# Block 1's attention: fewer chunks projected up front, a second buffer for the written parts, and operands loaded one head ahead

## The chip, the cores and the metric

The kernel runs on one core of one Trainium2 chip. The metric is the time of one execution on the device, in microseconds (us). The core has five engines that run side by side and wait for each other by semaphores: TensorE (PE, matmuls and transposes into PSUM), VectorE (DVE), ScalarE (ACT), GpSimd (POOL) and SyncE (SP), which here issues nearly all DMAs. PSUM has eight banks of 128 x 512 float32; the kernel calls them a to h.

## The reference, cut to what matters

Three blocks work one after the other on x, 512 tokens of 1024 features, float32. Each mixes tokens and then applies a feed-forward layer. The change lies in the mixer of the first block, which has two kinds of attention side by side:

```python
h = rms_norm(x, mix_norm[l])
proj = h @ w_in[l]
qa, ka, va, qb, kb, vb = [proj[..., offs[i]:offs[i + 1]] for i in range(6)]
...
oa = diff_attention(qa[:, :, 0], qa[:, :, 1], ka[:, :, 0], ka[:, :, 1], va, lam, rel_bias)
oa = rms_norm(oa, diff_subln[l]) * (1.0 - lambda_init)
...
qb = apply_rope(rms_norm(qb, q_norm[l]), cos, sin)   # shortened
kb = apply_rope(rms_norm(kb, k_norm[l]), cos, sin)   # shortened
ob = gqa_attention(qb, kb, vb)
x = x + jnp.concatenate([oa, ob], axis=-1) @ w_out[l]
```

There are 8 differential heads (two maps of scores each, with a bias by distance, whose difference weighs the values) and 8 grouped heads, four of which share one of two key and value heads. A head is 64 wide.

## The kernel before, in words

Activations lie with their features on the partitions, as eight chunks of [128, 512 tokens]. A matmul in float32 is made of three matmuls of float32r: each operand is cut into a high and a low part (hi on ACT, lo on DVE), and hi*hi + hi*lo + lo*hi is summed in PSUM (`mm3x`, L116 to L122). A weight panel comes by DMA into `wraw`, a ring of three, and is cut into `whi` and `wlo` at L137 and L138. A projection of one chunk (`proj`) is 8 x 3 = 24 matmuls of 512 columns.

`heads1` (L538 to L696) is the attention of block 1. Its order before the change:

1. The two grouped key heads are projected, normed and rotated (`rope(4, "kpd", "mm")`, function at L544).
2. For chunks 0 and 1, which are two heads of each kind: the differential q and k (`proj_q`, `proj_k`, L643 to L647) and the grouped q (`rope`) are projected, through the PSUM ring "mm" (banks a to f).
3. Sixteen heads follow in turns, a differential one (d) and a grouped one (g): d0, g0, d1, g1 and so on; chunk c holds the heads 2c and 2c+1. Within the heads stand the value projections (`v_tokens`, at the first grouped head, 192 matmuls of 320 columns through banks c to f) and the projections of chunks 2 and 3: q and k at the first grouped head of chunk c - 2, the grouped q at the second differential head of chunk c - 2. These use the kind "pj", bank h alone.

`AH = 2` (L39) says how many chunks are projected ahead.

The result of each of these projections is drained by DVE (`af` at L582, `rf` at L550), and `parts` (L463) writes its two parts to DRAM, to be set out anew on the partitions:

```python
hl = self.keep("hl", self.HL, F32R, w=1024).rearrange("p (a w) -> p a w", a=2)   # L466
nc.scalar.activation(hl[:, 0], f, AF.Copy)                                       # L468
nc.vector.tensor_sub(hl[:, 1], f, f32v(hl[:, 0]))                                # L469
d = self.dr.tile([128, 2, 512], F32, name=name, tag=name, bufs=4)                # L473
nc.sync.dma_start(out=d, in_=f32v(hl))                                           # L474
```

`HL = 1` (L40): there is one such buffer. (Block 3 sets it to 2 for itself at L1412.) A head's operands are then loaded from DRAM: `operand` (L585) makes `qd` and `kd` of a differential head by three DMAs each, from the ring "op1" of three buffers (L589 issues); `keys` (L568) loads the shared grouped keys, `kg`, two buffers, four DMAs at L573; the grouped q, `qg`, comes by two DMAs at L665. All of these are issued by SP, whose queue runs in order.

The heads are run by `attend` (L406). A head's four units (128 queries each) make the scores: for a differential head at L602, with bias and row minimum on DVE at L604 and the exponential on ACT at L460; for a grouped one at L626, L627 and L460. A head's unit runs ahead of the values of the head before: `values` (L429) transposes the weights on TensorE (L437, banks c and d), cuts them (`pth` L445, `ptl` L446) and multiplies them with the values (L447, L448, L441, banks e and f); `fold` (L456) adds the halves. A head's operands are loaded when its first unit is written (`lazy`, L634, calls `mk_diff` or `mk_gqa`).

After the heads stands the first half of the output's projection (`half_res`, L522), eight projections of 12 matmuls in bank h. Each is tied by `issue_after` (L531) behind a matmul of the heads' values, the first behind one of the tenth head, the last behind one of the sixteenth.

The order on each engine is not written out by hand. The kernel is a list of instructions whose place gives their priority; a scheduler with a model of their costs lays them out at build time, as their operands become ready in that model, and a tile waits until a buffer of its ring is free. So a projection can run well before or after its place in the list, but on each engine the order is then fixed, and an instruction that waits holds up all behind it.

Temporary tiles of 128 x 512 come from a ring of five, "u", and for four names (`dq`, `pf`, `ct`, `cacc`, used in block 2) from a ring of three, "v", both in one pool that lives through the whole kernel (L78 to L82).

Of the kernel before, what the change touches and what calls it, by code (L numbers as in the profile page):

```python
# [21 lines left out]
# vectors with a column or more per partition, that come in one array  # L22
# [11 lines left out]
class K:  # L34
# [4 lines left out]
    AH = 2  # L39
    HL = 1  # L40
# [37 lines left out]
    def t(self, name, dt=F32):  # L78
        """A [128, 512] tile that lives for a few instructions."""
        if name in self.SECOND:  # L80
            return self.tp.tile([128, 512], dt, name=name, tag="v", bufs=3)
        return self.tp.tile([128, 512], dt, name=name, tag="u", bufs=self.NU)  # L82

    def ld(self, name):
        """One that is loaded from DRAM, ahead of its use."""
        return self.tp.tile([128, 512], F32, name=name, tag="ld", bufs=self.NL)

    def tx(self, name):
        """The same in the place of the residual's parts, when those are done."""
        return f32v(self.keep(name, 16, F32R, self.xp, tag="x"))  # L90
# [15 lines left out]
    def psum(self, kind="mm"):  # L106
        """A bank of PSUM; kinds that share none don't wait for each other."""
        ring = self.BANKS[kind]
        tag = ring[self.turn.get(kind, 0) % len(ring)]
        self.turn[kind] = self.turn.get(kind, 0) + 1  # L110
        return self.ps.tile([128, 512], F32, name=tag, tag=tag, bufs=1)
# [12 lines left out]
    def weight(self, src, n, nk, own=0):  # L124
        """Load a weight panel [128, nk*128] and cut it into two parts."""
# [21 lines left out]
    def weight_bg(self, src):  # L147
        """The same for work beside the main line, 512 columns at a time."""
# [9 lines left out]
    def split_act(self, x, name, bufs, scale=None):  # L158
        """x (times a per-partition scale) into two float32r parts."""
# [12 lines left out]
    def rsqrt(self, p, w, scale, eps=EPS, own=False):  # L172
        """1/sqrt(p*scale + eps) of [128, w] sums, rounded like float32; eps may be a tile."""
# [7 lines left out]
        # the exponent and mantissa bits give log2 within 0.043; two Newton steps follow  # L181
# [7 lines left out]
    def tok_sums(self, st, s, ind, n, nq=4):  # L189
        """Sums over s's partitions by token: st[:, q*n + j] = sum_p s[p, q*128 + token] ind[p, j];  # L190
        s may be a list, whose sums are added."""
# [5 lines left out]
    def rows(self, r, kind="mm"):  # L197
        """[128 tokens, 4] -> the tokens' row on all partitions (PSUM)."""
# [5 lines left out]
    def head_rows(self, r, split, kind="mm"):  # L204
        """r[:, q, h] of some heads -> rows of a chunk whose partitions are (half, head, 32) or (head, d)."""
# [19 lines left out]
    def rstd(self, acc, dim=1024, kind="st", own=False):  # L225
        """1/sqrt(mean+eps) by token from the sums of squares acc, [128 tokens, 4]."""
# [4 lines left out]
    def on_rows(self, r, kind="mm"):  # L231
        """The same on all partitions, [128, 512 tokens]."""
# [10 lines left out]
    def feed_start(self, g):  # L243
        """The residual's chunks arrive one by one; the next phase gets them normed by g."""
# [14 lines left out]
    def feed_end(self):  # L259
        """The fed chunks, 1/sqrt(mean+eps) of each token by row and by column, the residual."""  # L260
# [18 lines left out]
    def aside(self, ph, f, *args):  # L279
        """Calls f with its tiles in the pool ph."""  # L280
# [13 lines left out]
    def start(self, g):  # L294
        """The kernel's input as a phase gets it, its chunks on chip; the first weights come before."""
# [69 lines left out]
    def bias_rows(self):  # L365
        """-rel_bias of every key - query in DRAM, one copy per partition."""
# [39 lines left out]
    def attend(self, heads):  # L406
        """Heads as (unit, values, odd, dst, done): unit(q) makes the scores of a query
        chunk and returns a function that gives the weights; a head's units run ahead of
        the values of the one before."""
# [19 lines left out]
    def values(self, pv, kc):  # L429
        """o += v^T p^T for one chunk of keys; both parts of v on o's rows."""  # L430
# [19 lines left out]
    def fold(self, o, odd, dst):  # L450
        """Sum of the two 64-row halves of o into the even or odd half of dst."""
# [6 lines left out]
    def soft(self, p, mx, sm, e):  # L458
        """exp(-p - max(-p)) with its row sums."""
# [3 lines left out]
    def parts(self, f, name, scale=None):  # L463
        """A chunk's two parts in DRAM, to be set out anew on the partitions."""
# [15 lines left out]
    def v_tokens(self, src, xhl, vt, rtok, nh):  # L480
        """Values with tokens on partitions, each head as (hi | lo)."""
# [40 lines left out]
    def half_res(self, ocs, gs, res):  # L522
        """The residual and the output's projection of the first halves of both kinds of heads, in DRAM."""
# [14 lines left out]
    def heads1(self, xhl, rb, rtok, gq, ind, ocs):  # L538
# [5 lines left out]
        def rope(c, name, kind="pj"):  # L544
            """Grouped attention's q (or its k): projection, norm, gain and rotation of a
            chunk, whose rows are the first halves of its two heads and then the second
            halves; both parts of it in DRAM."""
# [20 lines left out]
        def keys(kv):  # L568
            ds = []
            for i in range(2):  # L570
                t = self.keep("kg", 2, F32R)
# [5 lines left out]
        # values  # L577
# [7 lines left out]
        def operand(tag, d, r, order):  # L585
            """The two 32-row groups of a head as 96-row operands of both parts."""
            t = self.keep(tag, 3, F32R, tag="op1", w=1024).rearrange("p (r w) -> p r w", r=2)
# [4 lines left out]
        def diff_head(h, sms, q2, k2):  # L592
# [4 lines left out]
            def unit(q):  # L597
# [9 lines left out]
                def weights():  # L607
                    """The two maps' difference, times the first one's sum."""
# [39 lines left out]

        def mk_diff(c, r):
            if r == 1:  # L650
                qgd[c + self.AH] = rope(c + self.AH, "qpd") if c < 4 - self.AH else None
            return diff_head(2 * c + r, sms[c], operand("qd", qds[c], r, (0, 0, 1)), operand("kd", kds[c], r, (0, 1, 0)))

        def mk_gqa(c, r):
            if r == 0:
                if c == 0:
                    self.v_tokens(D["w1_v"], xhl, vt, rtok, 5)
                if c % 2 == 0:
                    kg[c // 2] = keys(c // 2)
                if c < 4 - self.AH:  # L660
                    proj_q(c + self.AH)
                    proj_k(c + self.AH)
            t = self.keep("qg", 2, F32R)
            for i in range(2):
                nc.sync.dma_start(out=f32v(t[64 * i:64 * i + 64]), in_=self.part_rows(qgd[c], i, 32 * r, [(64, 2), (1, 32)]))  # L665
            return gqa_head(r, sms[4 + c], t, kg[c // 2])

        kg = {}
# [16 lines left out]

        for c in range(self.AH):
            proj_q(c, "mm")
            proj_k(c, "mm")
            qgd[c] = rope(c, "qpd", "mm")
# [9 lines left out]
    def tok_proj(self, src, lhs, nk, n, ntok, evac, kind="mm"):  # L699
        """Tokens on partitions: [128 ntok, n] blocks of x @ w, w as the moving operand."""  # L700
# [11 lines left out]
    def mod_start(self):  # L712
        """silu of c and c_ctx, doubled, on all partitions."""
# [13 lines left out]
    def mod_step(self, m):  # L727
        """A chunk of c @ w_mod (and of c_ctx's), features on partitions."""
# [11 lines left out]
    def modulation(self):  # L740
        """silu(c) @ w_mod + b_mod for c and c_ctx, features on partitions."""
# [19 lines left out]
    def log_decay(self):  # L761
        """log_sigmoid of the decay logits on all partitions, [128, (direction, head)]."""
# [7 lines left out]
        # log1p(e) = 2 atanh(e / (2 + e))  # L770
# [16 lines left out]
    def ctx_normed(self):  # L787
        """The context, normed and modulated, in two parts, and the decays over its positions."""
# [25 lines left out]
        # decays over the context's positions, with k's scale  # L814
# [11 lines left out]
    def ctx_states(self, hl, dec):  # L826
        """The two states that the context leaves, per head [128 d, 128 e], in two parts."""
# [23 lines left out]
    def norm_mod(self, xs, gg, sh, scale_b):  # L851
        """h = x * gg * scale_b + sh, in two parts."""
# [12 lines left out]
    def acc_sq(self, acc, s, c):  # L865
        """The squares of 8 chunks added up, the last ones left apart."""
# [1164 lines left out]
```

## Time and profile before

| | before |
|---|---|
| median of 3 runs | 2702.98 us |
| lowest and highest | 2700.18 and 2704.9 us |
| span of the profiled execution | 2697.9 us |
| PE busy in that span | 2605.0 us |
| DVE busy | 1565.2 us |
| ACT busy | 1053.6 us |
| DMA, mean | 126 GB/s |
| mean granted clock of TensorE | 0.983 |

The span runs from the first to the last instruction of one profiled execution; the time of a run also holds what lies around it. That execution has no time of its own here; the median is 5.0 us above its span. "Busy" counts every instruction from its start to its end, and matmuls overlap, so PE's share is near full where it only waits a little. "PEclk" is the part of the full clock that TensorE was granted in a stretch. In a timeline, a line has start, length, engine, source line, operation, result and operands, and in brackets how long the engine was idle before and what ended it.

### The profile page before, as it was taken

The page shows a single profiled execution, that of the slowest core. Times are in us where ns is not written, and L with a number is a line of the kernel's source. Part 1 is how long each engine was busy: PE and PEld are TensorE (multiplying, and loading weights), DVE is VectorE, ACT ScalarE, POOL GpSimd, SP SyncE. Part 2 cuts the span into 40 slices and gives each one's busy share as a digit, 9 for nine tenths or more (in the row PEclk, how much of TensorE's full clock was granted, in tenths as well). Part 3 has the DMA queues.
Part 4 walks back from the last instruction along what each step waited for, and adds up shares of the span by engine and source line. Part 5 has one row for each costly group of instructions (what it writes and reads, how often), then busy time and mean ns, then how long its engine had stood idle before and what let it go on. Part 6 is the DMA issues. An engine that isn't in the chain of part 4 may idle for free.

```text
span 2697.9 us, 31194 instructions
## 1 busy us (share of the span) xinstructions
PE 2605.0 (97%) x11820; PEld 2105.4 (78%) x11820; DVE 1565.2 (58%) x2432; ACT 1053.6 (39%) x1604; POOL 409.4 (15%) x331
## 2 busy tenths in 40 slices
PE   8999998989999999899999899999999899999999
PEld 7887787767888887788788677888778777878787
DVE  7866645787544544577432554334545977747464
ACT  4222233676422324355323533223433464424232
POOL 1001012232000004133111301000200323101000
PEclk9999999999999999899999899999999999999999
DMA  5565644433532323431233343232524644322333
GB/s 196 179 200 193 204 153 147 135 100 122 197 95 94 94 93 103 149 110 66 96 100 133 109 143 97 95 94 94 172 78 149 198 113 154 102 94 92 97 93 110
DMA packets 114594, 340.00 MB, mean 126 GB/s; under 512 B 13784, under 2 KB 15768, under 8 KB 114314
## 3 DMA queue, kind: packets, MB, share of 16 engines
q1 hardware_dynamic: 104010, 301.02, 34.6%
q0 software_dynamic: 10432, 36.97, 4.5%
q8 instruction: 93, 1.52, 0.2%
q14 instruction: 59, 0.48, 0.1%
HBM read 301.47 MB, written 40.67 MB: 127 GB/s over the span
## 4 chain that ended last, share of the span: by engine, by line
PE 88%; DVE 5%; DMA 3%; ACT 2%; issue 1%; POOL 1%; SPq 0%; POOLq 0%; ACTq 0%; DVEq 0%
PE c L122 5%; PE a L122 5%; PE a L120 5%; PE e L122 5%; PE c L120 4%; PE e L120 4%; PE e L121 4%; PE a L121 4%; PE c L121 4%; PE b L122 4%; PE b L120 4%; PE b L121 4%; PE f L120 4%; PE f L121 4%; PE f L122 4%; PE d L120 4%
## 5 line engine op out<-in xcount | busy, mean ns | idle before, releaser
L137 ACT ACTIVATE whi<-wraw 128x1024 fp32r<-128x1024 f32 (+4 forms) x426 | 430.1, 1012 | 1050.6 <-PE a L121 183.5
L138 DVE TENSOR_TENSOR wlo<-wraw,whi 128x1024 fp32r<-128x1024 f32 (+5 forms) x410 | 494.0, 1207 | 355.3 <-ACT whi L137 335.4
L122 PE MATMUL e<-xh,wlo 128*128 128x512 f32 x368 | 143.9, 391 | 0.6 <-DVE wlo L138 0.6
L121 PE MATMUL e<-xl,whi 128*128 128x512 f32 x368 | 144.3, 392 | 0.0
L120 PE MATMUL e<-xh,whi 128*128 128x512 f32 x368 | 144.0, 391 | 0.0
L121 PE MATMUL a<-xl,whi 128*128 128x512 f32 x352 | 138.9, 395 | 4.6 <-DVE xl L169 4.6
L120 PE MATMUL a<-xh,whi 128*128 128x512 f32 x352 | 139.7, 397 | 0.5 <-ACT whi L137 0.5
L122 PE MATMUL a<-xh,wlo 128*128 128x512 f32 x352 | 138.8, 394 | 0.7 <-DVE wlo L138 0.7
L121 PE MATMUL c<-xl,whi 128*128 128x512 f32 x352 | 138.7, 394 | 0.0
L120 PE MATMUL c<-xh,whi 128*128 128x512 f32 x352 | 138.5, 393 | 0.0
L122 PE MATMUL c<-xh,wlo 128*128 128x512 f32 x352 | 138.2, 393 | 0.0
L120 PE MATMUL b<-xh,whi 128*128 128x512 f32 x304 | 120.6, 397 | 9.0 <-ACT xh L168 7.9
L122 PE MATMUL b<-xh,wlo 128*128 128x512 f32 x304 | 120.1, 395 | 1.8 <-DVE wlo L138 1.8
L121 PE MATMUL b<-xl,whi 128*128 128x512 f32 x304 | 120.0, 395 | 0.0
L165 ACT ACTIVATE hh<-h 128x512 fp32r<-128x512 f32 x98 | 61.8, 630 | 148.5 <-DVE h L344 92.6
L872 POOL TENSOR_TENSOR acc<-sq 128x512 f32<-128x512 f32 x11 | 15.4, 1402 | 665.9 <-ACT sq L271 388.9
L120 PE MATMUL f<-xh,whi 128*128 128x512 f32 x280 | 111.0, 396 | 1.6 <-ACT xh L860 1.6
L121 PE MATMUL f<-xl,whi 128*128 128x512 f32 x280 | 110.9, 396 | 0.4 <-DVE xl L861 0.4
L122 PE MATMUL f<-xh,wlo 128*128 128x512 f32 x280 | 110.5, 395 | 0.8 <-DVE wlo L138 0.8
L122 PE MATMUL d<-xh,wlo 128*128 128x512 f32 x272 | 106.6, 392 | 0.0
L121 PE MATMUL d<-xl,whi 128*128 128x512 f32 x272 | 106.4, 391 | 0.0
L120 PE MATMUL d<-xh,whi 128*128 128x512 f32 x272 | 106.4, 391 | 0.0
(1119 smaller groups left out, 6427.2 us busy)
## 6 DMA issues: line engine op xcount, KB each, us to landing
wraw<-w_up SPq DMA_DIRECT2D x76, 512.0 KB
mw<-w_mod POOLq DMA_DIRECT2D x48, 512.0 KB, 4.5
wraw<-ffn_w_gate SPq DMA_DIRECT2D x43, 512.0 KB
wraw<-ffn_w_up SPq DMA_DIRECT2D x43, 512.0 KB
wraw<-w_down SPq DMA_DIRECT2D x40, 512.0 KB
wraw<-ffn_w_down SPq DMA_DIRECT2D x32, 448.0 KB
wraw<-w_gate SPq DMA_DIRECT2D x24, 512.0 KB
wraw<-ffn_w_down SPq DMA_DIRECT2D x16, 512.0 KB
```

The costliest lines, as they stand in the source:

```text
L120: mm(out, ah, bh, start=(first and i == 0), stop=False)
L121: mm(out, ah, bl, start=False, stop=False)
L122: self.last_mm = mm(out, al, bh, start=False, stop=(last and i == n - 1)).ins
L137: nc.scalar.activation(hi[:, i:j], raw[:, i:j], AF.Copy)
L138: (nc.gpsimd if self.pool_lo else nc.vector).tensor_sub(lo[:, i:j], raw[:, i:j], f32v(hi[:, i:j]))
L165: nc.scalar.activation(hi, x, AF.Copy)
L872: i = (self.nc.vector if c == 6 else self.nc.gpsimd).tensor_add(a, acc, s).ins
```

## The change

The class constants `AH = 2` and `HL = 1` become `HL = 2`. In front of the heads only chunk 0 is projected, and its first head's operands are loaded at once. The next chunk's projections stand one chunk ahead among the heads: q at the first differential head, k at the first grouped head, the grouped q at the second differential head of the chunk before. Each differential head's building loads the operands of the grouped head behind it, and each grouped head's building those of the differential head behind it. The ring of `qd` and `kd` grows from three to four, that of `kg` from two to three. The ring "v" moves from the common pool to the pool of the phase that uses it. All comments are dropped.

```diff
-    AH = 2
-    HL = 1
+    HL = 2
...
         if name in self.SECOND:
-            return self.tp.tile([128, 512], dt, name=name, tag="v", bufs=3)
+            return self.ph.tile([128, 512], dt, name=name, tag="v", bufs=3)
...
         def keys(kv):
             ds = []
             for i in range(2):
-                t = self.keep("kg", 2, F32R)
+                t = self.keep("kg", 3, F32R)
...
         def operand(tag, d, r, order):
-            t = self.keep(tag, 3, F32R, tag="op1", w=1024).rearrange("p (r w) -> p r w", r=2)
+            t = self.keep(tag, 4, F32R, tag="op1", w=1024).rearrange("p (r w) -> p r w", r=2)
...
+        def ahead_diff(c, r):
+            ops[c, r] = operand("qd", qds[c], r, (0, 0, 1)), operand("kd", kds[c], r, (0, 1, 0))
+
+        def ahead_gqa(c, r):
+            if r == 0 and c % 2 == 0:
+                kg[c // 2] = keys(c // 2)
+            t = self.keep("qg", 2, F32R)
+            for i in range(2):
+                nc.sync.dma_start(out=f32v(t[64 * i:64 * i + 64]), in_=self.part_rows(qgd[c], i, 32 * r, [(64, 2), (1, 32)]))
+            ops[4 + c, r] = t
+
         def mk_diff(c, r):
-            if r == 1:
-                qgd[c + self.AH] = rope(c + self.AH, "qpd") if c < 4 - self.AH else None
-            return diff_head(2 * c + r, sms[c], operand("qd", qds[c], r, (0, 0, 1)), operand("kd", kds[c], r, (0, 1, 0)))
+            if c < 3:
+                if r == 0:
+                    proj_q(c + 1)
+                else:
+                    qgd[c + 1] = rope(c + 1, "qpd")
+            ahead_gqa(c, r)
+            return diff_head(2 * c + r, sms[c], *ops[c, r])
 
         def mk_gqa(c, r):
             if r == 0:
                 if c == 0:
                     self.v_tokens(D["w1_v"], xhl, vt, rtok, 5)
-                if c % 2 == 0:
-                    kg[c // 2] = keys(c // 2)
-                if c < 4 - self.AH:
-                    proj_q(c + self.AH)
-                    proj_k(c + self.AH)
-            t = self.keep("qg", 2, F32R)
-            for i in range(2):
-                nc.sync.dma_start(out=f32v(t[64 * i:64 * i + 64]), in_=self.part_rows(qgd[c], i, 32 * r, [(64, 2), (1, 32)]))
-            return gqa_head(r, sms[4 + c], t, kg[c // 2])
+                if c < 3:
+                    proj_k(c + 1)
+            if (c, r) != (3, 1):
+                ahead_diff(c + r, 1 - r)
+            return gqa_head(r, sms[4 + c], ops[4 + c, r], kg[c // 2])
+
+        ops = {}
...
-        for c in range(self.AH):
-            proj_q(c, "mm")
-            proj_k(c, "mm")
-            qgd[c] = rope(c, "qpd", "mm")
+        proj_q(0, "mm")
+        proj_k(0, "mm")
+        ahead_diff(0, 0)
+        qgd[0] = rope(0, "qpd", "mm")
```

## The prediction

> **What bounds the kernel now.** I read the page first.
>
> ```profile
> span 2697.9 us, 31194 instructions
> PE 2605.0 (97%) x11820; PEld 2105.4 (78%) x11820; DVE 1565.2 (58%) x2432; ACT 1053.6 (39%) x1604; POOL 409.4 (15%) x331
> ```
>
> TensorE is busy 97% of the span, so the kernel can only become shorter where TensorE stands still or runs slowly. The change touches block 1's attention alone, which lies between about 384 and 670 us. So I next read the stretches of that stage (columns: stretch, length, busy time and instructions of PE, PEld, DVE, ACT and POOL, granted clock, DMA share, GB/s).
>
> ```profile
> core 0: us, PE busy (x) PEld busy (x) DVE busy (x) ACT busy (x) POOL busy (x), PEclk, DMA share, GB/s
> 436.64:440.05 3.41, 3.41 (x15) 3.41 (x15) 0.00 (x0) 0.00 (x0) 0.00 (x0) 0.50 0.84 261
> 446.88:453.70 6.82, 5.85 (x22) 5.59 (x23) 3.00 (x8) 3.23 (x7) 1.10 (x1) 0.50 0.44 138
> 521.97:528.79 6.82, 6.82 (x26) 5.90 (x25) 5.09 (x16) 4.50 (x13) 2.85 (x2) 0.50 0.33 95
> 556.10:559.52 3.42, 3.42 (x8) 1.78 (x7) 3.41 (x15) 3.22 (x10) 0.93 (x2) 0.50 0.39 123
> 566.34:569.76 3.42, 3.25 (x12) 2.88 (x13) 2.96 (x10) 3.17 (x8) 0.50 (x1) 0.50 0.13 49
> 586.82:590.24 3.42, 3.42 (x10) 2.44 (x11) 3.21 (x12) 2.65 (x8) 0.00 (x0) 0.50 0.13 50
> 447.85:664.73 216.88, 201.95 (x1055) 156.54 (x1057) 176.79 (x431) 148.93 (x332) 70.19 (x52) 0.95 0.39 124
> 550.00:600.00 50.00, 39.78 (x200) 27.61 (x198) 45.85 (x125) 39.03 (x92) 22.64 (x17) 0.90 0.37 112
> 600.00:640.00 40.00, 39.81 (x223) 30.69 (x223) 36.60 (x89) 30.03 (x70) 14.91 (x11) 1.00 0.33 104
> ```
>
> Three things are to be seen. Six stretches run at half the granted clock; they lie in and behind the pauses of TensorE. From 550 to 600 us TensorE is busy for only 39.78 of 50 us, since no projection is left there to fill the pauses of the heads. And in the same 50 us DVE is busy 92%, so it is nearly a second bound. The chain of waits of TensorE then names the pauses (total us, times, longest).
>
> ```profile
> PE a L602 <- DMA qd<-qdd: 6.0, 1, 6.0
> PE a L602 <- DMA kd<-kdd: 3.9, 1, 3.9
> PE f L448 <- DVE ptl L446: 2.9, 5, 1.6
> PE e L120 <- DVE af L582: 2.6, 1, 2.6
> ...
> PE a L626 <- DMA kg<-kpd: 1.0, 1, 1.0
> ```
>
> The waits for qd and af stand before the first head, those for kd and kg between 574 and 586 us; the longest of the others here is 1.6 us.
>
> **The start of the heads.** Why does the first score (L602) wait? The SP queue, ACT and DVE in order of time show it.
>
> ```profile
> 419.68 0.33 SPq L474 DMA_DIRECT2D kpd<-hl  x1
> ...
> 424.07 0.43 SPq L474 DMA_DIRECT2D qdd<-hl  x1
> ...
> 434.98 1.00 SPq L474 DMA_DIRECT2D kdd<-hl  x1
> 443.99 1.26 SPq L589 DMA_DIRECT2D kd<-kdd  x3
> ...
> 517.72 0.32 SPq L474 DMA_DIRECT2D qpd<-hl  x1
> ```
>
> ```profile
> 422.37 0.63 ACT L468 ACTIVATE hl<-af 128x512 fp32r<-128x512 f32 x1 [1.13 <-DMA kpd<-hl]
> ...
> 444.03 0.63 ACT L468 ACTIVATE hl<-rf 128x512 fp32r<-128x512 f32 x1 [10.54 <-DMA kdd<-hl]
> ```
>
> ```profile
> 418.37 0.68 DVE L550 TENSOR_TENSOR rf<-d,rb 128x512 f32<-128x512 f32 x1
> ...
> 433.52 0.69 DVE L469 TENSOR_TENSOR hl<-af,hl 128x512 fp32r<-128x512 f32 x1 [3.77 <-ACT hl L468]
> ...
> 434.73 0.68 DVE L582 SCALAR_TENSOR_TENSOR af<-e,rb 128x512 f32<-128x512 f32 x1
> ```
>
> The written parts have one buffer, hl. Each chunk's parts can only be made when the chunk before has landed in DRAM: the shared keys' parts are written at 419.68, q's at 424.07, k's only at 434.98, after q's have landed. Loads of k follow at 443.99. Meanwhile DVE stands at L469 (433.52), and behind that instruction in its queue stands the emptying of bank e (434.73), for which the 2.6 us pause waits.
>
> With two buffers q's parts take the second one, and k's take the one that is free at 422.37. So k's parts stand where q's stand now, and their write starts at 424.07 instead of 434.98: 10.9 us earlier. What follows stays the same chain, so the first score comes at about 436.9 instead of 447.85. From the other side, the same gain counted as TensorE's lost time is 2.6 + 6.0 of waits, and half of the busy time at half clock, 3.41/2 + 5.85/2 = 4.6: 13.2 us. A write that shares the queues with q's write could land later: the trace has 2.7 us (419.68 to 422.37) and 9.0 us (434.98 to 443.99) for such a write, and does not show two in flight; I take the 9.0 that stands in the chain already. Term: 10.9, at most 13.2, and at least about 4 if two writes delay each other by most of a write (10.9 less the difference 6.3 of those two is 4.6).
>
> Is there work for TensorE until 436.9? These rows give its prices.
>
> ```profile
> 408.82 0.39 PE L120 MATMUL e<-xh,whi 128*128 128x512 f32 x1
> ...
> 414.27 0.39 PE L120 MATMUL f<-xh,whi 128*128 128x512 f32 x1
> ...
> 426.58 0.31 PE L120 MATMUL c<-whi,xh 128*128 128x320 f32 x1
> ...
> 429.22 0.31 PE L120 MATMUL c<-whi,xh 128*128 128x320 f32 x1
> ...
> 447.85 0.77 PE L602 MATMUL a<-kd,qd 96*128 96x512 f32 x1 [6.02 <-DMA qd<-qdd]
> ...
> 481.30 0.40 PE L602 MATMUL a<-kd,qd 96*128 96x512 f32 x1
> ...
> 489.18 0.48 PE L120 MATMUL h<-xh,whi 128*128 128x512 f32 x1
> ...
> 499.34 0.50 PE L120 MATMUL h<-xh,whi 128*128 128x512 f32 x1 [0.58 <-DVE rf L550]
> ...
> 526.13 1.20 PE L626 MATMUL a<-kg,qg 128*128 128x512 f32 x2
> ```
>
> A projection (24 matmuls) takes 414.27 - 408.82 = 5.45 us. After the change, four stand in front of the heads in banks a to d, ending at 408.8; three (16.4 us) go among the heads. From there to 436.9 are 28.1 us. The next pair's q projection (5.45, in bank h) and the value projections (18 matmuls from 426.58 to 429.22, so 0.147 each; 2 x 4 x 8 x 3 = 192 of them make 28.2) are 33.6 us of cover. They no longer wait for bank e and f, which now stay empty. Banks c and d are emptied by 418.37 plus 0.68; between 414.27 and then TensorE could be bare for up to 4.8 us if the values begin with bank c. That would not move the first score, which hangs on DMA, and I cost it at nothing; without the cover it would cost those 4.8 us.
>
> The two other projections of that pair (10.9 us of TensorE) come behind the first score, and the second half of the values (14.1 us), which runs behind it now, goes ahead of it. So the heads do not get fuller.
>
> **The loads one head ahead.** Pauses of 3.9 (kd) and 1.0 (kg) us are loads that are issued when the head before has freed the buffer. Four op1 buffers (two heads' q and k) and three kg buffers let the same DMAs be issued a head earlier; their number and bytes stay. With them goes the half clock behind the pause, 586.82 to 590.24: 3.42/2 = 1.7. Term: 6.6. What may be late next is the DMA's data itself, since on SP a load that waits for its write holds up what is queued behind it: weight panels (L144) and the next writes of parts (L474). The bound is one write, 0 to 9.0 us per chunk; I take 0, because the loads of a pair stand two heads behind its projections, and come back to it below.
>
> **Filling the pauses.** From 550 to 600 TensorE idles 10.2 us, 4.9 of them counted above. The other 5.3 and half of the two stretches from 556.10 and 566.34 (3.3) could be filled by the projections that now stand later. DVE says how much: it is at 92% there, and no more than that where TensorE is full (36.60 of 40 us from 600 to 640). I take 3 of 8.6; the ends are 0 and 12 (with half of the 6.82 from 521.97).
>
> On the clock a rule can be weighed. The Trainium skill ("TensorE: Matmul & The Clock Gate", Part 1: The HAM clock gate) says that the clock halves after an idle window of about 3.4 us, and that a busy one restores it. The lengths 3.41 and 6.82 agree; but the stretch from 521.97 lies where no wait of the list is longer than 1.6 us. By the rule alone every half-clock stretch in the heads would go with the two long pauses, 3.3 + 3.4 = 6.7 us more than I count; by the trace crowded short pauses halve it too, and I stay with the trace.
>
> The ring of three that moves from the common pool to the phases, the larger rings and the dropped comments add no instruction: 0, with 2 us either way for another placing.
>
> Sum: 10.9 + 6.6 + 3.0 = 20.5 us. The profiled span of 2697.9 becomes 2677.4; the median lies 5.1 above that span, so 2702.98 becomes **2682.5 us**.
>
> **The rivals.** First, *slower: the grouped queries come too late*. One pair ahead instead of two shortens the lead of the rotated query: it is projected in a head of the first kind and needed three heads later. From the row at 481.30, where that head begins, it takes 7.9 us until 489.18 (bank h is taken), 28.5 until the write at 517.72, 2.7 to 9.0 to land, and 3.9 for the load (443.99 to 447.85): 43.0 to 49.3. Three heads are now 3 x 216.88/16 = 40.7 and would be 38.9 (207.3/16, the heads shortened by 9.6). At the middle it is 7.3 us late, three times 22, with a half-clock stretch each (1.7) 27: 20.5 - 27 gives 2709.5. It decides where the path is longer than three heads. Against it: the order is by readiness, and the row at 499.34 is a projection that runs 26.8 us before the head in whose place it is written begins (526.13); so projections run ahead into pauses. 10%.
>
> Second, *only the start*: the heads are held by DVE, and the loads' pauses come back as waits for DVE. Then 10.9 remains: 2692.1. For it speaks the 92%. 20%.
>
> Third, *DVE packed as well as it ever is*: with fillers everywhere the 176.79 us of DVE work between 447.85 and 664.73 run at 92%, in 192.2 instead of 216.88 us: 24.7, and 10.9 at the start: 35.6, 2667.4. 12%.
>
> Fourth, *the second buffer does little*: both writes share the queues, k's lands 4.6 earlier at best, and a late load in the heads takes that back: 2703. 8%.
>
> **How the numbers follow.** My forecast (2682.5; by its ends 2673 to 2692) gets 50%. About 0.2%, 5.4 us, is what a measurement of this kernel can tell from no change. The forecast, the second and the third are faster: 82%, less 2 for a forecast that falls short. The fourth and that remainder are the same: 10%. Slower 10%. For the range I take in the third and the second, with a short fall of the latter: 2665 to 2699; the first and fourth rivals are left out.
>
> **What would show it.** Right: first score near 437 us; no wait of L468 for qdd or kdd before it; TensorE's waits for qd, kd and kg gone; projections in bank h still running past 550; no half clock between 436 and 454. Wrong: waits of L626 for qg (the first rival), or DVE still near 80% of the heads with TensorE's pauses as before.

## The result, and the profile after

| | before | after |
|---|---|---|
| median of the timed runs | 2702.64 us (4 runs) | 2723.53 us (4 runs) |
| lowest and highest | 2700.18 and 2704.9 us | 2716.54 and 2728.22 us |
| ratio after / before, 95% interval | | 1.0082 [1.0065, 1.01] |
| span of the profiled execution | 2697.9 us | 2724.0 us |

The kernel became 0.8% slower; the prediction had 2682.5 us. (The kernel before was timed once more beside it, hence 2702.64.) In the changed kernel the line numbers up to the scores are one lower: the differential scores are L601, the grouped ones L625, the operand loads L588, those of `kg` L572, the writes of parts L473; the loads of `qg` are L657. The page after:

```profile
span 2724.0 us, 31191 instructions
...
PE 2614.4 (96%) x11820; PEld 2112.3 (78%) x11820; DVE 1561.4 (57%) x2432; ACT 1054.6 (39%) x1604; POOL 406.8 (15%) x331
```

DVE's and ACT's work is the same as before within 4 us, so the loss is in pauses and clock. TensorE's waits between 395 and 700 us (total, times, longest):

```profile
PE a L625 <- DMA qg<-qpd: 15.9, 4, 6.3
PE a L601 <- DMA kd<-kdd: 9.3, 1, 9.3
PE b L625 <- ACT e L459: 2.5, 3, 1.7
```

The old waits for qd, af and kg are gone, and so is the wait for kd in the middle of the heads. A wait for kd before the first score and waits for qg at four grouped heads have taken their place. To see what this costs I split the stage at 460 us and end it at the first write of `xn`, the first result behind the attention (672.8 us before, 691.4 after). First before, then after; the columns are those of the prediction's stretches.

```profile
400.00:460.00 60.00, 50.70 (x255) 44.52 (x254) 29.70 (x61) 22.05 (x36) 13.23 (x13) 0.91 0.44 136
460.00:672.80 212.80, 196.52 (x1036) 150.02 (x1036) 172.59 (x416) 143.99 (x322) 65.31 (x47) 0.96 0.39 123
```

```profile
400.00:460.00 60.00, 50.75 (x291) 47.39 (x291) 30.45 (x66) 25.50 (x44) 11.93 (x11) 0.91 0.46 145
460.00:691.40 231.40, 199.59 (x996) 148.89 (x996) 170.09 (x411) 140.79 (x313) 64.33 (x50) 0.93 0.34 111
```

TensorE's pauses (length less busy time) were 9.3 + 16.3 = 25.6 us and are 9.3 + 31.8 = 41.1. The start has the same pause as before, and the heads have 15.5 us more. Its busy time in the heads rose by 3 us at a lower granted clock. Together that is the 18.6 us by which `xn` is late; the other 7.5 us of the 26.1 between the two spans come behind it, where the work is the same. That last stretch took between 2025 and 2036 us in the sixteen profiled executions of this case, and no run shows what moves it.

How the start went, on SP and TensorE in order of time:

```profile
418.94 0.33 SPq L473 DMA_DIRECT2D kpd<-hl  x1
419.55 0.33 SPq L473 DMA_DIRECT2D qdd<-hl  x1
421.63 1.66 SPq L572 DMA_DIRECT2D kg<-kpd  x3
423.40 0.74 SPq L473 DMA_DIRECT2D kdd<-hl  x1
...
434.39 1.25 SPq L588 DMA_DIRECT2D kd<-kdd  x3
```

```profile
433.21 0.31 PE L120 MATMUL e<-wlo,xh 128*128 128x320 f32 x1
442.77 0.77 PE L601 MATMUL a<-kd,qd 96*128 96x512 f32 x1 [9.25 <-DMA kd<-kdd]
...
443.76 0.47 PE L121 MATMUL e<-whi,xl 128*128 128x320 f32 x1
```

The second buffer did what the prediction said of it: k's parts are written at 423.40 (predicted: 424.07), 11.6 us earlier than before. But the load of kd is issued only at 434.39, since that write took eleven microseconds. The chain of waits shows such steps all through the heads (start, length, what was in flight):

```profile
418.94 2.62 DMA kpd<-hl
...
423.40 10.93 DMA kdd<-hl
...
436.63 9.62 DMA qd<-qdd
...
446.31 9.97 DMA qpd<-hl
...
456.91 9.31 DMA qg<-qpd
...
502.22 2.60 DMA qpd<-hl
...
505.40 7.48 DMA qg<-qpd
...
554.66 8.25 DMA qpd<-hl
```

A write of the same 512 KB takes 2.6 us or 8 to 11. What stands ahead of the long ones is a load of `kg` or `qg`: `kg` at 421.63 ahead of the write of 423.40. The trace also has the landings that each of these DMAs leaves on its semaphore; the table gives their number, and when the last one comes:

| issued at | DMA | landings | last one after |
|---|---|---|---|
| 418.94 | kpd<-hl (write) | 16 | 2.62 us |
| 419.55 | qdd<-hl (write) | 16 | 3.32 us |
| 421.63 | kg<-kpd (load) | 3 | 4.91 us |
| 422.28 | kg<-kpd (load) | 3 | 8.45 us |
| 422.82 | kg<-kpd (load) | 3 | 10.26 us |
| 423.40 | kdd<-hl (write) | 16 | 10.93 us |
| 424.27 | qd<-qdd (load) | 16 | 10.47 us |

Each load of `kg` leaves three landings, the first about 1 us after its issue and two at its end; all others leave 16. Of the 16 of the write of 423.40, fourteen come by 3.04 us, like those of a short write, and the last two at 10.44 and 10.93 us. The load of 424.27 shows the same: fourteen by 4.01 us, the last two at 9.85 and 10.47. So it is two sixteenths of these transfers that are late, as many as a load of `kg` has landings at its end. A stretch in which only loads of `qg` are under way says the same; its last three figures are the granted clock, the share of the 16 DMA engines' time, and GB/s:

```profile
625.00:629.40 4.40, 0.00 (x0) 0.00 (x0) 1.20 (x3) 0.81 (x2) 2.83 (x2) 0.67 0.13 49
```

0.13 is 2 of 16. These loads are written with a source whose outermost dimension is 2, `[(64, 2), (1, 32)]`; those of `qd` and `kd` have 32 outermost, `[(1, 32), (32, 2)]`. The Trainium skill ("DMA: Bandwidth & Descriptors", Why a DMA increments its semaphore by 16 and not by 1) states that a DMA goes to as many engines, at most 16, as divide the slowest dimension of both its sides. The landings and the share of 0.13 agree with it.

### The profile page after: what moved, and what is told of

The parts are those of the page before. It is cut to its first block, busy times and chain, and to the rows that moved or that the text cites. A ratio compares the mean times of both kernels' runs of the same rounds, so it can differ in the third digit from the quotient of the medians.

```text
span 2724.0 us, 31191 instructions
## 1 busy us (share of the span) xinstructions
PE 2614.4 (96%) x11820; PEld 2112.3 (78%) x11820; DVE 1561.4 (57%) x2432; ACT 1054.6 (39%) x1604; POOL 406.8 (15%) x331
## 4 chain that ended last, share of the span: by engine, by line
PE 79%; issue 8%; DMA 5%; DVE 5%; ACT 2%; POOL 1%; SPq 0%; POOLq 0%; ACTq 0%; DVEq 0%
PE b L121 4%; PE b L120 4%; PE b L119 4%; PE d L119 4%; PE d L120 4%; PE d L121 4%; PE f L121 4%; PE f L120 4%; PE f L119 4%; PE a L119 4%; PE c L119 4%; PE a L120 4%; PE c L120 4%; PE c L121 4%; PE a L121 4%
## 5 line engine op out<-in xcount | busy, mean ns | idle before, releaser
L119 PE MATMUL b<-xh,whi 128*128 128x512 f32 x384 | 152.0, 396 | 10.2 <-ACT xh L167 6.8
L121 PE MATMUL b<-xh,wlo 128*128 128x512 f32 x384 | 151.4, 394 | 0.8 <-DVE wlo L137 0.8
L120 PE MATMUL b<-xl,whi 128*128 128x512 f32 x384 | 151.4, 394 | 0.0
L120 PE MATMUL d<-xl,whi 128*128 128x512 f32 x344 | 134.8, 392 | 2.6 <-DVE xl L168 2.6
L121 PE MATMUL e<-xh,wlo 128*128 128x512 f32 x280 | 110.2, 394 | 1.9 <-DVE wlo L137 1.9
L119 PE MATMUL e<-xh,whi 128*128 128x512 f32 x280 | 110.7, 395 | 0.0
L120 PE MATMUL a<-xl,whi 128*128 128x512 f32 x272 | 108.5, 399 | 2.0 <-DVE xl L168 2.0
L120 PE MATMUL e<-xl,whi 128*128 128x512 f32 x280 | 110.0, 393 | 0.0
L119 PE MATMUL a<-xh,whi 128*128 128x512 f32 x272 | 108.4, 398 | 0.0
L121 PE MATMUL a<-xh,wlo 128*128 128x512 f32 x272 | 107.6, 396 | 0.0
```

The costliest lines, as they stand in the source:

```text
L119: mm(out, ah, bh, start=(first and i == 0), stop=False)
L120: mm(out, ah, bl, start=False, stop=False)
L121: self.last_mm = mm(out, al, bh, start=False, stop=(last and i == n - 1)).ins
```

## The experiments

Three theories. **A**: the grouped queries are rotated too late, as one pair ahead is too short a lead (the prediction's first rival). **B**: the early loads crowd SP's queue. **C**, formed after the first four runs: the loads of `kg` and `qg` sit on two DMA engines; they are late themselves, and whatever needs all 16 engines stands behind them. Each experiment's ratio is to the kernel before, timed on the same chip.

**e1: two chunks up front again.**

```diff
-            if c < 3:
-                if r == 0:
-                    proj_q(c + 1)
-                else:
-                    qgd[c + 1] = rope(c + 1, "qpd")
+            if r == 1 and c < 2:
+                qgd[c + 2] = rope(c + 2, "qpd")
...
-                if c < 3:
-                    proj_k(c + 1)
+                if c < 2:
+                    proj_q(c + 2)
+                    proj_k(c + 2)
...
+        proj_q(1, "mm")
+        proj_k(1, "mm")
+        qgd[1] = rope(1, "qpd", "mm")
```

> The changed kernel with one part undone: two chunks are projected up front again, and the others stand where they stood before; two buffers for the written parts and the loads one head ahead stay. Theory A (the grouped query comes too late, because its projection has only one chunk of lead): TensorE's waits of the grouped scores for qg, 15.9 us in four in the changed kernel, fall under 2 us, and the time falls by those and their half-clock stretches, 20 to 30 us below the changed kernel: 2694 to 2704. Theory B (the loads one head ahead crowd the SP queue and the DMA queues): the waits for qg or kd stay, and the time stays within 8 us of the changed kernel, 2716 to 2732.

2712.87 us, ratio 1.0042 [1.0027, 1.0057], between the ranges of the two theories. No wait for qg is left, but this one is:

```profile
PE b L601 <- DMA kd<-kdd: 13.7, 1, 13.7
```

So A explains about half, and something else keeps the kernel slower than before.

**e2: the second buffer alone.** In the kernel before, `HL = 1` becomes `HL = 2`.

> The kernel before with one part alone: two buffers for the written parts. Both theories let it be faster: k's parts are written about 11 us earlier and the loads stand where they stood, so the first score comes 7 to 11 us earlier than 447.85 and the time falls by 5 to 11 us: 2692 to 2698. If, as in the changed kernel, the load of k takes 8 us instead of 4 and the values are queued behind the first score, it gains 0 to 5 us: 2698 to 2703.

2713.98 us, ratio 1.0045 [1.003, 1.006]. Neither theory expected this: the one edit that the prediction credited with 10.9 us costs 12 by itself.

```profile
PE b L602 <- DMA kd<-kdd: 11.6, 1, 11.6
PE a L626 <- DMA kg<-kpd: 4.8, 1, 4.8
```

**e3: grouped queries that are never late.**

```diff
-   ... in_=self.part_rows(qgd[c], i, 32 * r, [(64, 2), (1, 32)]))
+   ... in_=self.part_rows(qgd[0], i, 32 * r, [(64, 2), (1, 32)]))
```

> The changed kernel, but the grouped queries of all four chunks are loaded from chunk 0's copy in DRAM, which was written long before; every projection is still made and written, and loads and bytes are the same. So the output of the grouped heads of chunks 1 to 3 is that of other queries. Theory A: the waits for qg go, but for the first head's 2.9 us, and 18 to 28 us with them: 2696 to 2706. Theory B: as many loads in the same places, so no more than 6 us less: 2717 to 2728.

2708.51 us, ratio 1.0026 [1.0014, 1.0037], 15 us below the changed kernel, still above the one before, and again between the two ranges. Of the 15.9 us of waits for qg 3.6 are left; the wait for kd at the start stayed (9.9 us), as in the changed kernel.

**e4: one pair up front alone.** In the kernel before, `AH = 2` becomes `AH = 1`.

> The kernel before with one part alone: one chunk projected up front, the others one chunk ahead (q and k at the first grouped head, the grouped q at the second differential head of the chunk before); one buffer for written parts, loads at the head itself. Theory A: the grouped queries are late here too, by more than in the changed kernel since writes are in a row and loads come at the head: waits for qg of 15 to 40 us, 2715 to 2745. Theory B: no loads ahead, so no loss: 2695 to 2708.

2724.0 us, ratio 1.0085 [1.0067, 1.0103], in A's range. The grouped scores wait; "issue" stands where the profile names nothing that ended the wait, but a load of `qg` lands 0.1 to 0.2 us before the end of both:

```profile
PE a L626 <- issue: 10.5, 2, 8.2
...
PE a L626 <- DMA qg<-qpd: 4.9, 1, 4.9
```

Up to here A has its waits, but it cannot say why e2 is slow. That led to the landings above and to theory C. Its test changes how two loads are written, nothing else.

**e5: the changed kernel with `kg` and `qg` loaded over 16 engines.**

```diff
-   ... self.part_rows(d, i, 32 * kv, [(64, 2), (1, 32)]))       # keys
+   ... self.part_rows(d, i, 32 * kv, [(1, 32), (64, 2)]))
...
-   ... self.part_rows(qgd[c], i, 32 * r, [(64, 2), (1, 32)]))   # qg
+   ... self.part_rows(qgd[c], i, 32 * r, [(1, 32), (64, 2)]))
```

> This is the changed kernel with the loads of kg and qg written with the dimension of 32 rows outermost instead of the dimension of 2 heads (the 64 rows of a head come in another order on the partitions, in q and k alike, so that the scores stay the same). In the traces so far these loads put their packets on two of the 16 DMA engines and take 7 to 9 us; the loads of qd and kd, whose outermost dimension is 32, put theirs on 16. Theory C (the slow loads of kg and qg are themselves late, and hold up every write of parts and every load of kd that comes behind them): qg takes some 3 us, the writes 2.6, the wait for kd at the first score falls from 9.3 to under 3, the first score comes at 436 to 439, of the 15.9 us of waits for qg under 4 are left; 2680 to 2698 us. Theory A alone (the rotation ends too late, whatever the loads take): the waits for qg lose only what one load is shorter by, about 1 us each, and the time stays above 2717 us. Theory B (too many loads in SP's order): the order is the same, so the time is that of the changed kernel, 2723, within 5.

2694.46 us, ratio 0.9977 [0.9965, 0.9988]: by the ratios (from 1.0082) some 28 us gone, by the order of two dimensions. The start, on SP and TensorE:

```profile
421.45 0.33 SPq L473 DMA_DIRECT2D kpd<-hl  x1
...
424.14 1.89 SPq L572 DMA_DIRECT2D kg<-kpd  x3
426.12 0.53 SPq L473 DMA_DIRECT2D kdd<-hl  x1
...
430.03 1.32 SPq L588 DMA_DIRECT2D kd<-kdd  x3
```

```profile
436.44 0.47 PE L601 MATMUL a<-kd,qd 96*128 96x512 f32 x1 [0.42 <-issue]
```

The write of k now takes 3.2 us (16 landings) and the first score comes at 436.44 after a pause of 0.42 us. A load of `qg` takes this long at least, in the middle and at most, in a view that covers six of the sixteen; by the landings all of them take 2.6 to 3.6 us:

```profile
DMA to landing us min/median/max: 2.6/2.7/3.0
```

```profile
PE a L625 <- DMA qg<-qpd: 1.8, 1, 1.8
```

Of 15.9 us of waits for qg, 1.8 are left. C's numbers came out, but for the write (2.6 us expected). A alone had said that the time stays above 2717, B that it stays at 2723: both fall. In the chain of the changed kernel the write of the rotated queries had taken 2.6 to 10.0 us and the load behind it 7.5 to 9.3; with both short, the same lead is enough but for those 1.8 us.

**e6, e7, e8: the same edit in the other versions.** e6 is the kernel before, e7 is e1 and e8 is e2, each with the two loads spread.

> The same other order of the rows in the kernel before, and nothing else. Theory C: the writes and loads at the start of the heads no longer stand behind the load of kg (the load of kd of the first chunk took its turn after it), the first score comes some 3 to 6 us earlier than 447.85 and the later waits for kg and kd (4.9 us in all) go; 2690 to 2698 us. Without C, the kernel's waits for qd, kd and kg are a matter of when they are asked for, and the time stays at 2702, within 3.

> The changed kernel with two chunks projected up front, as in the kernel before, and the other order of the rows: what is left of the change is the second buffer for written parts and the loads one head ahead. Without the other order this took 2713, with a wait of 13.7 us for the first kd. Theory C: that wait falls under 4 us, the time is 2680 to 2695 and below that of the kernel before with the other order, since the pauses between the heads go too. Against C: the second buffer and the early loads make the queue itself longer, the wait for kd stays above 8 us and the time above 2705.

> The kernel before with two buffers for written parts and the other order of the rows. Without the other order the second buffer made it 12 us slower (2714; the load of the first kd, 11.6 us late, stood behind the load of kg). Theory C: the second buffer now gives what the prediction said of it, the write of k no longer waits for that of q; the first score comes before that of the kernel before with the other order; 2682 to 2694 us. Against C: the second buffer itself costs, and the time stays above 2705.

e6: 2693.43 us, ratio 0.9975 [0.9963, 0.9986]. e7: 2699.44, 1.0003 [0.999, 1.0015]. e8: 2698.48, 0.9998 [0.9987, 1.0008]. All gain, as C says: by the ratios 7, 11 and 13 us. But e7 and e8 end no lower than the kernel before, above C's ranges. In e6 the first score comes at 439.91, 7.9 us earlier than before and more than the 3 to 6 expected. The chain of waits of the kernel before and then of e6 shows what the prediction had in front of it:

```profile
422.88 0.60 SPq L573
...
423.52 0.50 SPq L573
...
424.07 8.77 DMA qdd<-hl
...
434.98 8.94 DMA kdd<-hl
```

```profile
422.56 0.59 SPq L573
...
423.20 0.59 SPq L573
...
423.84 4.33 DMA qdd<-hl
...
430.30 4.98 DMA kdd<-hl
```

L573 is the load of `kg`. The same two loads stand ahead of the same write, and it takes 8.77 us in one kernel and 4.33 in the other.

For e8 against e6, TensorE's stretches; e6 first:

```profile
400.00:460.00 60.00, 54.22 (x299) 48.29 (x298) 36.78 (x77) 27.07 (x49) 16.50 (x15) 0.97 0.51 163
460.00:660.70 200.70, 187.38 (x991) 141.25 (x990) 165.53 (x401) 139.43 (x310) 61.59 (x46) 0.97 0.39 122
```

```profile
400.00:460.00 60.00, 57.51 (x335) 51.90 (x334) 38.20 (x82) 29.73 (x51) 19.56 (x16) 1.00 0.60 191
460.00:667.80 207.80, 190.56 (x951) 140.64 (x950) 163.20 (x396) 136.88 (x306) 57.91 (x44) 0.94 0.35 108
```

The second buffer fills the start (pauses 2.5 instead of 5.8 us), and the heads lose it: pauses 17.2 instead of 13.3, and a clock of 0.94 instead of 0.97 over some 200 us, about 6 us. Some 36 to 39 of its matmul records have moved from the heads to the start (335 and 951 instead of 299 and 990). I read the loss as work that is missing there as a filler; no run tests this by itself.

**e9: only `kg` spread, in the changed kernel.**

> The changed kernel with the other order of rows in the loads of kg alone; the loads of qg keep theirs, so that q and k of the grouped heads no longer match row by row and the scores of those heads are those of a k whose rows are permuted (same shapes, same instructions). It splits what spreading both loads gave (29 us). Theory C: the load of kg alone holds up the first kd, so the first score comes at 436 to 439 instead of 442.8, and the loads of qg still take 7 to 8 us each, so that most of the waits for qg stay (10 to 16 us) and the time is 2706 to 2717. If instead the load of kg was the whole of it, the waits for qg go as well and the time is near 2694; if the loads of qg were the whole of it, the time is near 2723 and the first score stays at 442.

2705.22 us, ratio 1.0022 [1.0009, 1.0035], just below C's range. The first score comes without a wait for kd, and of the waits for qg 6.0 us are left, fewer than the 10 to 16 expected: some of them too had come from `kg`. By the ratios `kg` was worth 0.60% (16 us) and `qg` 0.45% (12 us).

**e10, e11, e12: parts of the change on the spread loads.** e10 is e5 with `HL = 1`. e11 is e6 with the loads one head ahead, their larger rings and the move of the ring "v". e12 is e5 with the rotation at the first differential head, q at the first grouped head and k at the second differential head.

> The changed kernel with both loads spread over 16 engines and one buffer for written parts instead of two. By the prediction's own sum the second buffer brings the first score forward by one write (now 4 us), and taking it away costs up to 4: first score 440 to 443, 2696 to 2700 us. By what the kernel before showed with the loads spread (2693.4 with one buffer, 2698.5 with two), an earlier first score only moves value projections behind it, and the second buffer brings nothing: 2688 to 2695 us, although the first score comes later.

> The kernel before with both loads spread, one buffer, two chunks up front, and only the loads one head ahead (with the buffers that they need) taken from the change. The waits for loads in the heads of the kernel before with the loads spread are 1.1 us (qd) in one place and nothing at kd and kg, so early loads have little left to gain: 2690 to 2695 us against its 2693.4. If the early loads shorten the pauses between heads as the prediction had it (3 us beside 6.6 for the waits), it takes 2684 to 2690. If they crowd SP's order (theory B), it takes 2696 or more.

> The changed kernel with both loads spread, and the three pieces of the next chunk set out among the heads in another order: the grouped queries' rotation first (in the first differential head), then the projection of q, then that of k. With the loads spread 1.8 us of waits for qg are left. If the late rotation still costs more than that wait (through what it does to the clock in the half of the loop that follows), this takes 2686 to 2691 us; if not, 2692 to 2697 as the changed kernel with the loads spread; if it makes q or k of the differential heads late in turn, over 2700 with waits for qd or kd.

e10: 2692.19 us, ratio 0.9968 [0.9954, 0.9983], in the range of "the second buffer brings nothing". e12: 2697.81, 0.9996 [0.9982, 1.0009]; the wait for qg is gone, and a wait of 2.6 us for kd and one of 1.8 for qd have come: just above the middle case of its expectation, with the beginnings of the third. e11: 2702.99, 1.0018 [1.0003, 1.0033], above e6 by 9.6 us in the medians and 12 by the ratios. That is the number which theory B gave, but not by B's mechanism: no DMA is among TensorE's longer waits. It is the clock:

```profile
400.00:460.00 60.00, 54.67 (x297) 49.03 (x296) 36.79 (x74) 26.65 (x46) 14.88 (x14) 0.94 0.55 171
460.00:675.50 215.50, 201.30 (x995) 150.56 (x994) 168.69 (x404) 140.83 (x313) 61.98 (x46) 0.90 0.36 112
```

The pauses are 19.5 us, as in e6 (19.1). But 10% of 215.5 us instead of 3% of 200.7 are lost to the clock: 21.6 against 6.0, and the first `xn` is 14.8 us later (675.5 against 660.7). These two executions lie further apart than the medians (2707.36 and 2689.81 us), so they overstate the loss. Over all ten runs of each the mean granted clock is 0.9801 against 0.9834; of 2700 us that is 8.9, nearly all of the 9.6 between the medians.

**e13, e14: the move of "v" alone, and one pair up front alone, on the spread loads.**

> The kernel before with both loads spread and only the move of the three scratch tiles to the other pool, which makes room for the early loads. If the move is what cost 9.6 us beside the early loads, this takes 2701 to 2705 us; if the early loads are (by the order of the instructions that they bring about, and the clock), it stays at 2693.4, within 3.

> The kernel before with both loads spread and only one pair of heads projected up front (one buffer, loads at the head itself). Without the other order of rows this took 2724, with 15.4 us of waits at the grouped scores. If those waits came from the slow loads, as in the changed kernel, they fall under 5 us and the time is 2688 to 2698; if the rotation itself is late (theory A, the loads being asked for at the head), over 8 us of them stay and the time is 2705 to 2720.

e13: 2691.13 us, ratio 0.9959 [0.994, 0.9978]. The move costs nothing, so e11's loss belongs to the early loads with their larger rings, and to the order of instructions that they bring about. e14: 2700.3, 1.0001 [0.9987, 1.0015], by the ratios 23 us below e4, with no wait for qg among the longer ones: here too the grouped queries were late because of the slow DMAs. It lies a little above its range.

All versions side by side, as ratios to the kernel before:

| version | two engines | 16 engines |
|---|---|---|
| before | 1 | 0.9975 (e6), 0.9959 with the move of "v" (e13) |
| second buffer alone | 1.0045 (e2) | 0.9998 (e8) |
| early loads alone | not run | 1.0018 (e11) |
| second buffer and early loads | 1.0042 (e1) | 1.0003 (e7) |
| one pair up front alone | 1.0085 (e4) | 1.0001 (e14) |
| one pair up front and early loads | not run | 0.9968 (e10) |
| the whole change | 1.0082 | 0.9977 (e5) |

All five versions that were run both ways gain from the spread loads. The whole change costs 0.82% with the loads on two engines and 0.02% with them on 16 (0.9977 against 0.9975, intervals that overlap): its loss comes from the loads on two engines, and beside that it brings nothing. No part of it beats the kernel before with spread loads by more than the intervals. e5, e6, e10 and e13 beat both kernels that the prediction was about; between them the intervals overlap.

## Why the prediction was wrong

Two steps failed: the prices of the write and the load at the start of the heads, by which the 10.9 us were to be gained, and the 0 for data that come late, which is most of the loss.

**The start of the heads.** The step that failed is "what follows stays the same chain": the write of k at 9.0 us and its load at 3.9, moved forward as a block. The prediction had two rows for such a write, 2.7 and 9.0 us. It weighed only a second write on the same queues as a reason, and took the 9.0. But both long writes of the kernel before (8.77 and 8.94 us) had loads of `kg` under way in front of them, the last of which landed at 440.46, and these use two engines. Writes do not hold each other up by much: in the changed kernel the writes at 418.94 and 419.55 were in flight together and took 2.6 and 3.3 us. Moved forward, the write of k fell close behind three of those loads. From it to the issue of its load 11.0 us passed instead of 9.0, and the load took 8.4 instead of 3.9 (434.39 to 442.77). The first score came at 442.77, not 436.9, and nothing was left of the 10.9: up to 460 us the pauses are 9.3 us and the clock 0.91, before as after.

With the loads spread the first score came at 436.44. That this is so near to 436.9 is luck. Counted from the write of the keys' parts (421.45 there, 419.68 before) it came after 15.0 us, and by the sum after 17.3: from the write of k to the next issue 3.9 us passed instead of 9.0, and the load took 6.4 instead of 3.9.

The cover failed beside it. The 33.6 us of projections and values were there, but only those up to 433.21 stood ahead of the first score in TensorE's order. The next value matmul, for bank e, was queued behind the waiting score and ran at 443.76. So the first score moved by 5.1 us and the pause before it did not shrink: 9.25 us against 2.6 + 6.0.

**The loads one head ahead.** The waits for kd and kg in the heads did go, as the step said. Yet they were no matter of being asked for late: in e6 they are gone too, with the loads at their old place, so spreading the loads alone took that term. The second step that failed stands here too. That DMA data might be late was bounded by 9.0 us a chunk and taken as 0. It came to 15.9 us in four waits for qg, about the 15.5 us by which the pauses of the heads grew; e3, in which 3.6 of them are left, is 15 us faster.

**Filling the pauses.** Predicted 3 us. In e5, with the loads spread, the pauses of the heads are larger than before: from the rows below 18.4 us in 202.9, against 16.3 in 212.8, while the start has 0.4 against 9.3.

```profile
400.00:460.00 60.00, 59.58 (x347) 54.26 (x347) 37.24 (x77) 30.02 (x53) 15.38 (x12) 1.00 0.64 193
460.00:662.90 202.90, 184.54 (x953) 135.89 (x953) 163.73 (x400) 136.80 (x305) 61.33 (x48) 0.97 0.35 113
```

The like-for-like pair is e5 and e6, the two kernels with spread loads: at the start e5 has pauses of 0.4 us instead of 5.8, in the heads 18.4 instead of 13.3. What the start gains, the heads lose; as with e8, that the missing work is the cause is my reading.

**The second rival**, "only the start", had 2692.1 us, and e5 comes to 2694.5. That is luck. e6 reaches 2693.4 with none of the change, and e10 2692.2 without the second buffer that the rival's 10.9 us rest on. So the gain of e5 is that of the loads. Nor do the waits show DVE holding the heads, as the rival had it: it is busy for 163.73 of e5's 202.9 us there, and TensorE's largest sum of waits for one of its lines is 2.6 us.

**The first rival** had the right signature, waits of L626 (now L625) for qg, and the right sign, and fell 14 us short (2709.5 against 2723.53). Its price for the path, 43.0 to 49.3 us, let the write land in 2.7 to 9.0 us and the load take 3.9; in the chain of the changed kernel the load took 7.5 to 9.3. It got 10%, since the forecast leaned on projections running ahead into pauses. It too stands on the slow loads: with them spread, the same lead is long enough but for 1.8 us in e5, and in e14 no wait for qg is among the longer ones.

**The clock.** That it halves without a long pause too, as the prediction held, is borne out by e11. The rule that the prediction weighed, that the clock halves after an idle window of about 3.4 us, is that of the Trainium skill ("TensorE: Matmul & The Clock Gate", Part 1: The HAM clock gate); the measurement differs from it. These are three stretches of e11, and TensorE's longest waits from 540 to 600 us:

```profile
520.00:560.00 40.00, 37.39 (x171) 26.12 (x171) 29.35 (x76) 22.39 (x52) 12.54 (x10) 0.84 0.34 99
560.00:600.00 40.00, 35.48 (x134) 24.29 (x134) 32.97 (x88) 28.42 (x68) 13.60 (x11) 0.70 0.35 105
553.50:573.98 20.48, 18.03 (x46) 10.76 (x45) 17.97 (x48) 13.88 (x36) 9.69 (x9) 0.50 0.39 112
```

```profile
PE g L195 <- ACT sq L271: 1.4, 1, 1.4
PE b L626 <- ACT e L460: 1.2, 2, 0.7
```

For 20.48 us on end the clock is 0.50, and from 540 to 600 us no pause is longer than 1.4 us. That crowded short pauses are the cause, as the prediction said, is not shown. What exactly halves the clock in such a stretch, and why e11 has more of them than e6 at the same sum of pauses, stays open; no run changed the clock by itself.

## What to carry to other kernels

When the same transfer stands in a trace at 2.7 and at 9.0 us, find out what was in flight beside the long one before moving it; a long price in a chain is a sign of contention, and a change that moves the transfer changes the price. Look at how many DMA engines each small load uses: a share of 0.13 with transfers under way and waits behind them are the sign, and putting a larger dimension outermost (with the same order of rows on both sides of the product) was worth 7 to 28 us here. Of work that shall cover a wait, check that it stands ahead of the waiting instruction in its engine's order.

## What the runs showed of the hardware

- A load of 128 KB whose outermost dimension is 2 used two of the 16 DMA engines, at 49 GB/s, and its neighbours that need all 16 waited for it: writes of 512 KB took 8 to 11 us instead of 2.6 to 3.3, with fourteen of their 16 landings in time and two late (14 by 3.04 us, the last at 10.93). With 32 outermost the same bytes took 2.6 to 3.6 us.
- The granted clock over some 200 us of heads lay between 0.90 (e11) and 0.97 (e6) at the same sum of TensorE's pauses, 19 us; in these two executions that is worth 15 us. In e11 it was 0.50 for 20.48 us on end, in which no wait of TensorE's was longer than 0.7 us.
